# Raw weight blocks of five quads in one ring tile, block by block, with accumulating transfers over two neighbouring quads

## The chip, the cores and the metric

The kernel runs on one core of one Trainium2 chip. The metric is device time in microseconds (us) for one execution; three runs of the kernel before gave 1760.03, 1761.9 and 1763.46, median 1761.9. One more execution was profiled. The five engines of the core are TensorE (PE; its weight loads are PEld), VectorE (DVE), ScalarE (ACT), GpSimd (POOL) and SyncE (SP); each runs its own instructions in order. POOL and SP also issue DMAs.

## The reference, cut to what matters

One decoder layer on x of 256 x 2048 in float32. What matters here are the large products with weights, since nearly all of the time is theirs:

```
x = x + 0.5 * (silu(h @ w_gate) * (h @ w_up)) @ w_down      # first FFN, 2048 -> 5632 -> 2048
q, k, v, ... = rmsnorm(x) @ w_in                            # attention and mLSTM, 256 positions
x = x + concat(y_A, y_B) @ w_out
x = x + 0.5 * (silu(h @ w_gate) * (h @ w_up)) @ w_down      # second FFN, the same shapes
out = rmsnorm(x)
```

## The kernel before, in words

**One product.** Every float32 operand is split into a high and a low part: `wh` is a rounded copy made on ACT (L132), `wl` the rest, made on DVE (L133). A block of weights of 128 x 512 is multiplied as high x high, high x low and low x high: two matmuls with `wh` (L181, L182), one with `wl` (L184). The split parts of 1024 columns are one pair of tiles of the pool `wsp`; four pairs are there, so ACT and DVE can be at most four pairs ahead of PE.

**Quads.** `Paired` computes two neighbouring column chunks, `wa` and `wb` (gate and up, or two chunks of the down projection), over the same activations. For its first `ns` pairs of 128 rows it takes seven products for the eight of a 2 x 2 block of weights, a *quad*, by sums of blocks. A quad holds three raw blocks of 128 x 512: block 0 is the first row block of `wa`, blocks 1 and 2 are the two row blocks of `wb`; the second row block of `wa` comes later, as `late` (L511), for two quads at once. The sums:

- T1 (L479, DVE): block 0 becomes block 0 + block 1, block 1 becomes block 2 + block 1, in one instruction.
- T2 (L495, or L497): block 0 becomes block 0 + block 2.
- T3 (L533): block 0 becomes block 0 + `late`.

T3 is always an accumulating DMA from POOL, 128 rows of 2048 bytes for each quad. T2 is one where `by_dma` holds (the gate and up chunks, and the wide ones in the middle of the layer, which have five quads) and its two quads aren't the last ones; otherwise DVE makes it.

**Order.** Quads are handled by twos (`twos`: 0 and 1, 2 and 3, then 4 alone). `leading` loads, splits and multiplies block 0 as it came (A1), makes T1, and for the two quads before splits block 0 again (S1) and makes T2. `sums` then splits block 0 after T2 (S2), issues T3 behind it, multiplies the bare `late` blocks, and the sums in block 1 (S3). `second` takes blocks 0 and 2 of each quad together, after T3. Units of plain products and the work of the chunk before are woven in between. A scheduler places each instruction on its engine by priority; splits and loads have the same high priority, and the engines keep the order in which it put them.

**Queues.** Raw blocks are loaded by POOL (L446 block 0, L208 through `load_pair` blocks 1 and 2 as rows of 4096 bytes; the first chunks by SP), plain units and `late` by SP. A quad's tile is one of five of the pool `wr`, tag `raw`, 6144 bytes in each partition.

Of the kernel before, what the change touches and what calls it, by code (L numbers as in the profile page):

```python
# [9 lines left out]
F32 = mybir.dt.float32  # L10
# [3 lines left out]
ALU = mybir.AluOpType  # L14
# [3 lines left out]
P = 128  # L18
# [6 lines left out]
CW = 512  # L25
# [7 lines left out]
UK = 2  # L33
# [16 lines left out]
ON_POOL = 3  # L50
FIRST_SUMS = 3
FLUSH = 3

SEEDED = N11, N21 = "n11", "n21"

# [5 lines left out]
def tile_trunk_layer(ctx: ExitStack, tc: tile.TileContext, x, xt, par, bias_if, lamv, fnorm,  # L61
                     wg1, wu1, wd1, wqk0, wqk1, wqk2, win, wout, wg2, wu2, wd2, out):
    nc = tc.nc
# [1 line left out]
    big = ctx.enter_context(tc.tile_pool(name="big", bufs=1))  # L65
    slots = ctx.enter_context(tc.tile_pool(name="slots", bufs=22))
    work = ctx.enter_context(tc.tile_pool(name="work", bufs=8))
    wr = ctx.enter_context(tc.tile_pool(name="wr", bufs=5))
    wrp = ctx.enter_context(tc.tile_pool(name="wrp", bufs=5))
    wsp = ctx.enter_context(tc.tile_pool(name="wsp", bufs=4))  # L70
    small = ctx.enter_context(tc.tile_pool(name="small", bufs=2))
    ps_acc = ctx.enter_context(tc.tile_pool(name="ps_acc", bufs=4, space=PSUM))
    ps_tr = ctx.enter_context(tc.tile_pool(name="ps_tr", bufs=2, space=PSUM))

    wqk = [wqk0, wqk1, wqk2]
    uid = [0]

    def nm(s):
        uid[0] += 1
        return f"{s}_{uid[0]}"  # L80
# [69 lines left out]
    def split_weights(src, hi, lo):  # L150
        made = split(src, hi, lo)
        for late, q, past in zip(made, queued, ahead):
            while q and len(splits) >= q[0][0]:
                past.append(q.pop(0)[1])
            del past[:-3]
            for early in past:
                after(late, early)
        return made


    def pair_tiles(pool, tag, shape):
        return (pool.tile(shape, F32R, tag=tag + "h", name=nm(tag + "h")),
                pool.tile(shape, F32R, tag=tag + "l", name=nm(tag + "l")))
# [36 lines left out]
    def flush(n=None):  # L200

        now = pending[:n]
        del pending[:n]
        for f in now:
            f()

    def load_pair(dst, w, k, queue=nc.sync):
        queue.dma_start(dst, w[k // LK][:, k % LK:k % LK + 2, :])  # L208

    def load_unit(w, k, pieces=(UK,), spare=False):  # L210
        n = w.shape[3]
        if spare:
            raw = wr.tile([P, 3, n], F32, tag="raw", name=nm("raw"))[:, 0:UK, :]
        else:
            raw = wrp.tile([P, UK, n], F32, tag="rawp", name=nm("rawp"))
        with tc.high_priority(offset=AHEAD):
            o = k % LK
            for m in pieces:
                nc.sync.dma_start(raw[:, o - k % LK:o - k % LK + m, :], w[k // LK][:, o:o + m, :])
                o += m  # L220
        return raw
# [3 lines left out]
    def in_turn(load):  # L225
        for early in turns[-1:]:
            after(load, early)
        turns.append(load)

    def tile_by_tile(w, ahead):  # L230
        raw = wr.tile([P, 3, w.shape[3]], F32, tag="raw", name=nm("raw"))
        hi, lo = pair_tiles(wsp, "w", [P, UK, w.shape[3]])
        with tc.high_priority(offset=AHEAD):
            for t in range(UK):
                ahead(0, t)
                in_turn(nc.sync.dma_start(raw[:, t, :], w[0][:, t, :]))
                made = split_weights(raw[:, t, :], hi[:, t, :], lo[:, t, :])
        splits.append(made)
        ahead(1)
        return hi, lo  # L240

    def units(accs, xp, w, nk, last_units=1, ahead=None, w0=0, banks=None):
# [16 lines left out]
        for u in range(nu):  # L259
            if u == FLUSH:  # L260
                flush()
# [123 lines left out]
    def wk(name):  # L385
        return work.tile([P, CW], F32, tag="w", name=nm(name))
# [11 lines left out]
    def soon(extra=40):  # L398
        return tc.high_priority(offset=AHEAD + extra)

    class Early:


        def __init__(self, engine):
            self.engine = engine
# [16 lines left out]
    class Paired:  # L422

        def __init__(self, xp, wa, wb, nk, ns, w0=0, queue=nc.gpsimd, by_dma=True):

            self.queue, self.by_dma = queue, by_dma and ns > 3
            self.xp, self.wa, self.wb, self.k0 = xp, wa, wb, w0 * LK
            self.ns, self.rest = ns, range(2 * ns, nk, UK)
            self.twos = [range(j, min(j + 2, ns)) for j in range(0, ns, 2)]

            self.n = wa.shape[3]
            self.off = self.n - wb.shape[3]
            self.raws = []

        def job(self, acc, j, xi, w, wi, first, last, on=False):
            xh, xl = self.xp[j][2 * (xi // 4):][:2]
# [2 lines left out]

        def load(self, j):  # L440
            n, off = self.n, self.off
            raw = wr.tile([P, 3, n], F32, tag="raw", name=nm("raw"))
            self.raws.append(raw)
            k = self.k0 + 2 * j
            with tc.high_priority(offset=AHEAD):
                self.queue.dma_start(raw[:, 0, :], self.wa[k // LK][:, k % LK, :])  # L446
                load_pair(raw[:, 1:3, off:], self.wb, k, self.queue)
                if off:
                    nc.gpsimd.memset(raw[:, 1:3, 0:off], 0.0)
# [38 lines left out]
        def second_sum(self, js):  # L488

            self.part(js, self.d, S1, 0, True, True)  # L490
            with tc.high_priority(offset=AHEAD):
                for j in js:
                    raw = self.raws[j]
                    if self.by_dma and js != self.twos[-1]:
                        nc.gpsimd.dma_start(raw[:, 0, :], raw[:, 2, :], accum_op=ALU.add)  # L495
                    else:
                        nc.vector.tensor_tensor(out=raw[:, 0, :], in0=raw[:, 0, :], in1=raw[:, 2, :], op=ALU.add)  # L497

        def copied(self, src, t, slack=SLACK - 1):
# [21 lines left out]
        def sums(self, gently):  # L521

            ds = self.copied(self.d, wk("ds"))
            lates = []
            for js in self.twos:
                lates.append((js, self.late(js)))
                self.part(js, self.x, S2, 0)
                if gently or self.rest[0] // UK not in self.xp:
                    with tc.issue_after(newest[0].ins):
                        flush(1)  # L530
                with tc.high_priority(offset=AHEAD):
                    for i, j in enumerate(js):
                        nc.gpsimd.dma_start(self.raws[j][:, 0, :], lates[-1][1][:, i, :], accum_op=ALU.add)  # L533
                if js[-1] == self.ns - 1:
                    us = self.copied(self.x, wk("us"))
                    with soon():
                        ahead_of_splits(1, nc.vector.tensor_tensor(out=self.d, in0=self.d, in1=us, op=ALU.subtract))
                if len(lates) > 1:
                    self.bare(*lates.pop(0))
            for js, raw in lates:  # L540
                self.bare(js, raw)
            for js in self.twos:
                self.part(js, self.x, S3, 1)
            self.n21 = self.copied(self.x, seeded(N21), SLACK - 2)
            with soon():
                ahead_of_splits(1, nc.vector.tensor_tensor(out=self.x, in0=ds, in1=self.x, op=ALU.subtract))
# [492 lines left out]
    for hb in range(NT):  # L1039
        for h in range(NH):  # L1040
            i = hb * NH + h
# [226 lines left out]
```

## Time and profile before

| | |
|---|---|
| median of three runs | 1761.9 us |
| the profiled execution | 1759.56 us |
| its span, first to last instruction | 1757.8 us |
| PE busy | 1744.6 us, 99% |
| DVE busy | 1617.8 us, 92% |
| ACT busy | 1267.4 us, 72% |
| POOL busy | 429.3 us, 24% |
| queue of POOL's DMAs, share of the 16 DMA engines | 45.1% |
| queue of SP's DMAs, share of the 16 DMA engines | 38.0% |

The first rows are from the times, the others from the profile's page. Busy time counts an instruction's own time; matmuls overlap, so a busy PE is not PE at its peak. PE's clock was granted in full (0.999 of it over the run).

### The profile page before, as it was taken

To read this page: it belongs to the slowest core of one execution; us is meant where nothing else is said; L and a number is where in the kernel's file an instruction comes from. 1 tells how busy PE (TensorE), PEld (TensorE's weight loads), DVE (VectorE), ACT (ScalarE), POOL (GpSimd) and SP (SyncE) were. 2 spreads that over 40 slices of the span, in tenths; PEclk is the share of its full clock that TensorE was granted. 3 is DMA by queue.
4 is the path that set the end of the run, shared out by engine and by line. 5 is a ranking of instruction groups with operands and counts; after the bars stand their busy time and mean duration, and the time that the engine had idled before them with its cause. 6 is when DMAs were issued, how large, how long until landed. Compare 5 with 4: busy or idle time off the path is not lost.

```text
span 1757.8 us, 24486 instructions
## 1 busy us (share of the span) xinstructions
PE 1744.6 (99%) x7926; PEld 1437.7 (82%) x7926; DVE 1617.8 (92%) x2189; ACT 1267.4 (72%) x1949; POOL 429.3 (24%) x630
## 2 busy tenths in 40 slices
PE   9999999999999999999999999999999999999998
PEld 7788888888888888987888888888888878888886
DVE  7999999999999999898888999999999999999997
ACT  8666777777677768777687777776777677677765
POOL 0022332322233312012231101122332332233310
PEclk9999999999999999999999999999999999999999
DMA  9787998999799977577886667898998999799973
GB/s 365 251 254 209 259 261 265 253 292 265 218 262 258 263 252 204 185 230 221 236 238 192 209 210 211 260 265 233 258 260 268 241 268 276 232 246 256 283 254 115
DMA packets 155265, 429.72 MB, mean 244 GB/s; under 512 B 17632, under 2 KB 18944, under 8 KB 154880
## 3 DMA queue, kind: packets, MB, share of 16 engines
q0 software_dynamic: 76304, 196.66, 45.1%
q1 hardware_dynamic: 77680, 229.40, 38.0%
q10 hardware_dynamic: 1152, 2.09, 0.3%
q8 instruction: 62, 1.02, 0.2%
q14 instruction: 67, 0.55, 0.1%
HBM read 349.56 MB, written 2.10 MB: 200 GB/s over the span
## 4 chain that ended last, share of the span: by engine, by line
PE 93%; DMA 2%; DVE 2%; issue 1%; ACT 0%; POOL 0%; SPq 0%; POOLq 0%; DVEq 0%; ACTq 0%
PE acc L184 18%; PE acc L181 18%; PE acc L182 18%; PE accn L181 12%; PE accn L182 12%; PE accn L184 12%; DVE wl L133 1%; DMA raw<-in_wg_dram 1%; PE tr L373 1%; DMA raw<-in_wu_dram 1%; PE tr L314 0%; PE sc L1060 0%; DMA rawp<-in_wg_dram 0%; ACT wh L132 0%; PE num L1011 0%
## 5 line engine op out<-in xcount | busy, mean ns | idle before, releaser
L132 ACT CAST wh<-raw 128x512 fp32r<-128x512 f32 (+2 forms) x885 | 601.5, 708 | 214.5 <-PE acc L182 66.3
L133 DVE TENSOR_TENSOR wl<-raw,wh 128x512 fp32r<-128x512 f32 (+2 forms) x885 | 676.1, 793 | 58.4 <-ACT wh L132 54.5
L132 ACT CAST wh<-rawp 128x1024 fp32r<-128x1024 f32 (+3 forms) x308 | 318.2, 1035 | 109.5 <-PE acc L182 55.1
L133 DVE TENSOR_TENSOR wl<-rawp,wh 128x1024 fp32r<-128x1024 f32 (+3 forms) x308 | 367.1, 1197 | 32.0 <-ACT wh L132 29.8
L181 PE MATMUL acc<-wh,xs 128*128 128x512 f32 (+2 forms) x956 | 369.5, 387 | 0.0
L182 PE MATMUL acc<-wh,xs 128*128 128x512 f32 (+2 forms) x956 | 368.9, 386 | 0.0
L184 PE MATMUL acc<-wl,xs 128*128 128x512 f32 (+2 forms) x956 | 317.6, 387 | 0.8 <-DVE wl L133 0.7
L533 POOL DMA_DIRECT2D raw<-late x176 | 152.6, 1053 | 442.7 <-DVE wl L133 422.9
L181 PE MATMUL acc<-wh,xt 128*128 128x512 f32 (+2 forms) x564 | 218.4, 388 | 0.7 <-ACT wh L132 0.7
L182 PE MATMUL acc<-wh,xt 128*128 128x512 f32 (+2 forms) x564 | 217.3, 386 | 0.0
L181 PE MATMUL accn<-wh,xt 128*128 128x512 f32 (+1 forms) x552 | 215.3, 391 | 0.0
L182 PE MATMUL accn<-wh,xt 128*128 128x512 f32 (+1 forms) x552 | 214.7, 390 | 0.0
L479 DVE TENSOR_TENSOR raw<-raw 128x1024 f32<-128x1024 f32 x176 | 211.0, 1217 | 0.8
L184 PEld LDWEIGHTS acc<-wl,xs 128*128 128x128 f32 x956 | 178.3, 188 | 39.2 <-DVE wl L133 3.6
L181 PEld LDWEIGHTS acc<-wh,xs 128*128 128x128 f32 x956 | 179.5, 188 | 36.4 <-ACT wh L132 0.6
L182 PEld LDWEIGHTS acc<-wh,xs 128*128 128x128 f32 x956 | 179.6, 188 | 35.6
L181 PE MATMUL accn<-wh,xs 128*128 128x512 f32 (+1 forms) x408 | 162.6, 400 | 1.9 <-ACT wh L132 1.9
L182 PE MATMUL accn<-wh,xs 128*128 128x512 f32 (+1 forms) x408 | 158.0, 388 | 0.0
L184 PE MATMUL acc<-wl,xt 128*128 128x512 f32 (+2 forms) x564 | 157.6, 386 | 0.0
L495 POOL DMA_DIRECT2D raw<-raw x92 | 78.9, 899 | 322.1 <-DVE wl L133 234.7
L184 PE MATMUL accn<-wl,xt 128*128 128x512 f32 (+1 forms) x552 | 154.7, 388 | 0.0
L184 PE MATMUL accn<-wl,xs 128*128 128x512 f32 (+1 forms) x408 | 140.9, 388 | 0.0
(229 smaller groups left out, 2125.0 us busy)
## 6 DMA issues: line engine op xcount, KB each, us to landing
rawp<-in_wd_dram SPq DMA_DIRECT2D x88, 512.0 KB, 5.6
raw<-late POOLq DMA_DIRECT2D x174, 256.0 KB, 5.3
raw<-in_wu_dram POOLq DMA_DIRECT2D x80, 512.0 KB, 8.4
rawp<-in_wu_dram SPq DMA_DIRECT2D x73, 512.0 KB, 5.1
rawp<-in_wg_dram SPq DMA_DIRECT2D x69, 512.0 KB, 5.2
raw<-raw POOLq DMA_DIRECT2D x92, 256.0 KB, 4.1
raw<-in_wd_dram POOLq DMA_DIRECT2D x44, 512.0 KB, 8.6
late<-in_wg_dram SPq DMA_DIRECT2D x41, 512.0 KB, 9.2
```

Of the source, the lines that this page charges most:

```text
L132: return (nc.scalar.copy(hi, src), nc.vector.tensor_tensor(out=lo, in0=src, in1=hi.bitcast(F32), op=ALU.subtract))
L133: nc.vector.tensor_tensor(out=lo, in0=src, in1=hi.bitcast(F32), op=ALU.subtract))
L181: nc.tensor.matmul(acc, lh, rh, start=first, stop=False, skip_group_check=on)
L182: nc.tensor.matmul(acc, ll, rh, start=False, stop=False, skip_group_check=on)
L184: newest[:] = [nc.tensor.matmul(acc, lh, rl, start=False, stop=last, skip_group_check=on)]
L373: nc.tensor.transpose(tr[:, i, hb * P:(hb + 1) * P], hs[hb][:, k * P:(k + 1) * P], ident)
L479: nc.vector.tensor_tensor(out=raw[:, 0:2, :], in0=raw[:, 0:3:2, :], in1=raw[:, 1:2, :].to_broadcast([P, 2, n]), op=ALU.add)
L495: nc.gpsimd.dma_start(raw[:, 0, :], raw[:, 2, :], accum_op=ALU.add)
L533: nc.gpsimd.dma_start(self.raws[j][:, 0, :], lates[-1][1][:, i, :], accum_op=ALU.add)
```

## The change

The five tiles of `wr` become one tile `ring` of [128, 3, 5, 512]: all five blocks 0 lie behind each other, then the five blocks 1, then the five blocks 2. A counter gives each quad the next of five places. A quad is a strided view of the ring. Two quads in neighbouring places have their blocks 0 in one stretch of 4096 bytes, and so their blocks 2; `late` of two quads is such a stretch already. Where the places of two quads follow each other, T2 and T3 of both are one accumulating DMA; where the first of them has place 4 and the second place 0, they stay two. The load of blocks 1 and 2 still reads 4096 bytes in a row, but writes two rows of 2048 bytes.

```diff
-    wr = ctx.enter_context(tc.tile_pool(name="wr", bufs=5))
+    wr = ctx.enter_context(tc.tile_pool(name="wr", bufs=1))
+    ring = wr.tile([P, 3, RAWS, CW], F32, name="ring")
+    turn = [0]
+    def raw_place():
+        turn[0] += 1
+        return (turn[0] - 1) % RAWS
+    def raw_tile(n):
+        return ring[:, :, raw_place(), 0:n]
...
+        def added(self, js, dst, srcs):
+            p = self.places[js[0]]
+            if len(js) == 2 and self.places[js[1]] == p + 1:
+                nc.gpsimd.dma_start(ring[:, dst, p:p + 2, 0:self.n], srcs, accum_op=ALU.add)
+            else:
+                for i, j in enumerate(js):
+                    nc.gpsimd.dma_start(self.raws[j][:, dst, :], srcs[:, i, :], accum_op=ALU.add)
...
-                    if self.by_dma and js != self.twos[-1]:
-                        nc.gpsimd.dma_start(raw[:, 0, :], raw[:, 2, :], accum_op=ALU.add)
+                if self.by_dma and js != self.twos[-1]:
+                    p, q = (self.places[j] for j in js)
+                    if q == p + 1:
+                        self.added(js, 0, ring[:, 2, p:p + 2, 0:self.n])
...
-                    for i, j in enumerate(js):
-                        nc.gpsimd.dma_start(self.raws[j][:, 0, :], lates[-1][1][:, i, :], accum_op=ALU.add)
+                    self.added(js, 0, lates[-1][1])
```

In the built program 34 of the 46 twos of T2 become one DMA, and 51 twos of T3; 24 DMAs of T2 and 74 of T3 stay as they were. POOL issues 85 DMAs fewer, 514 for 599. The other engines keep their instructions.

On POOL, one gate and up chunk of the first FFN, from the last loads of its quads to its last T3 (the numbers behind raw and late are tiles). Before:

```order
L446 DMA raw_2266<-in_wg_dram 128x512
L208 DMA raw_2266<-in_wu_dram 128x1024
L495 DMA raw_2176<-raw_2176 128x512
L495 DMA raw_2179<-raw_2179 128x512
L495 DMA raw_2214<-raw_2214 128x512
L495 DMA raw_2217<-raw_2217 128x512
L533 DMA raw_2176<-late_2323 128x512
L533 DMA raw_2179<-late_2323 128x512
L533 DMA raw_2214<-late_2339 128x512
L533 DMA raw_2217<-late_2339 128x512
L533 DMA raw_2266<-late_2365 128x512
```

and now:

```order
L470 DMA ring<-in_wg_dram 128x512
L221 DMA ring<-in_wu_dram 128x2x512
L452 DMA ring<-ring 128x1024 x2
L452 DMA ring<-late_2286 128x1024
L452 DMA ring<-late_2301 128x1024
L455 DMA ring<-late_2326 128x512
```

Each two of T2 and of T3 is one instruction, behind the split of its second quad.

On DVE, a chunk of the second FFN, where the low parts for S2 are made (the last `wl` of the four is that of the second two's second quad; xs is a low part of activations, sg a step of the gate). Before:

```order
L133 TENSOR_TENSOR wl_14017<-raw_13867,wh_14016 128x512
L133 TENSOR_TENSOR wl_14017<-raw_13870,wh_14016 128x512
L133 TENSOR_TENSOR wl_14033<-raw_13905,wh_14032 128x512
L133 TENSOR_TENSOR xs_13782<-xsum_13778,xs_13782 128x512
L395 SCALAR_TENSOR_TENSOR sg_13861<-acc_13469,rstd_10608,sg_13861 128x512
L133 TENSOR_TENSOR wl_14033<-raw_13908,wh_14032 128x512
```

and now:

```order
L146 TENSOR_TENSOR wl_13791<-ring,wh_13790 128x512 x2
L146 TENSOR_TENSOR xs_13563<-xsum_13559,xs_13563 128x512
L146 TENSOR_TENSOR wl_13806<-ring,wh_13805 128x512
L408 SCALAR_TENSOR_TENSOR sg_13642<-acc_13259,rstd_10452,sg_13642 128x512
L146 TENSOR_TENSOR wl_13806<-ring,wh_13805 128x512
```

The third `wl` and the step on xs have changed places; this is so in four chunks, and nowhere else has DVE's order changed. PE and ACT keep theirs. On SP two loads of plain units in the second chunk of the program stand behind two loads of raw blocks instead of ahead of them.

## Rows read from the trace of the kernel before

**Rows 1.** Busy time by stretch: length, then PE, PEld, DVE, ACT, POOL; clock, DMA share, GB/s.

```profile
60.00:1700.00 1640.00, 1639.24 (x7472) 1353.99 (x7472) 1523.40 (x2043) 1188.04 (x1820) 419.86 (x608) 1.00 0.85 245
```

**Rows 2.** POOL's timeline, one gate and up chunk: start, us, instruction, idle before and releaser.

```profile
237.17 0.86 POOL L495 DMA_DIRECT2D raw<-raw  x1 [0.86 <-DVE wl L133]
239.50 0.85 POOL L495 DMA_DIRECT2D raw<-raw  x1 [1.48 <-DVE wl L133]
241.24 0.84 POOL L495 DMA_DIRECT2D raw<-raw  x1 [0.89 <-DVE wl L133]
244.56 3.46 POOL L533 DMA_DIRECT2D raw<-late  x4 [2.48 <-DVE wl L133]
```

**Rows 3.** ACT's timeline, the same chunk.

```profile
242.44 1.14 ACT L132 CAST wh<-raw 128x512 fp32r<-128x512 f32 x2
243.79 0.63 ACT L132 CAST wh<-raw 128x512 fp32r<-128x512 f32 x1 [0.21 <-DMA raw<-raw]
244.32 0.58 ACT L503 COPY ds<-acc 128x512 f32<-128x512 f32 x1
244.99 0.62 ACT L132 CAST wh<-raw 128x512 fp32r<-128x512 f32 x1
...
253.62 1.05 ACT L132 CAST wh<-raw 128x1024 fp32r<-128x1024 f32 x1
```

**Rows 4.** DVE's timeline, the same chunk.

```profile
248.71 0.68 DVE L133 TENSOR_TENSOR wl<-raw,wh 128x512 fp32r<-128x512 f32 x1
```

**Rows 5.** PE's timeline, the same chunk.

```profile
250.19 0.39 PE L184 MATMUL acc<-wl,xs 128*128 128x512 f32 x1
```

**Rows 6.** All T2 by DMA (L495): us from issue to landing.

```profile
DMA to landing us min/median/max: 3.3/4.1/8.2
```

**Rows 7.** DMA queues: packets, MB, share of 16 engines.

```profile
q0 software_dynamic: 76304, 196.66, 45.1%
q1 hardware_dynamic: 77680, 229.40, 38.0%
```

**Rows 8.** Loads by L208 on POOL: duration ns min/median/max, first and last start.

```profile
L208 POOL DMA_DIRECT2D raw<-in_wu_dram x80: 530/537/571, 150.2 to 1631.7; - x80
...
L208 POOL DMA_DIRECT2D raw<-in_wqk_dram x2: 714/728/741, 643.3 to 645.6; - x2
```

**Rows 9.** POOL, ACT, DVE and PE timelines, a chunk at 1110 us.

```profile
1111.12 0.86 POOL L495 DMA_DIRECT2D raw<-raw  x1 [0.90 <-DVE wl L133]
...
1116.27 0.62 ACT L132 CAST wh<-raw 128x512 fp32r<-128x512 f32 x1 [0.15 <-DMA raw<-raw]
...
1119.99 0.68 DVE L133 TENSOR_TENSOR wl<-raw,wh 128x512 fp32r<-128x512 f32 x1
...
1120.87 0.39 PE L184 MATMUL acc<-wl,xs 128*128 128x512 f32 x1
```

**Rows 10.** The same four timelines, a chunk at 1420 us.

```profile
1421.38 0.84 POOL L495 DMA_DIRECT2D raw<-raw  x1 [0.89 <-DVE wl L133]
...
1426.26 0.62 ACT L132 CAST wh<-raw 128x512 fp32r<-128x512 f32 x1 [1.20 <-DMA raw<-raw]
...
1429.97 0.68 DVE L133 TENSOR_TENSOR wl<-raw,wh 128x512 fp32r<-128x512 f32 x1
...
1430.71 0.50 PE L184 MATMUL acc<-wl,xs 128*128 128x512 f32 x1
```

**Rows 11.** POOL, DVE and PE timelines, a chunk at 1462 us.

```profile
1462.59 0.85 POOL L495 DMA_DIRECT2D raw<-raw  x1 [0.90 <-DVE xsum L344]
...
1467.50 0.75 DVE L395 SCALAR_TENSOR_TENSOR sg<-acc,rstd,sg 128x512 f32<-128x512 f32 x1
1468.16 0.68 DVE L133 TENSOR_TENSOR wl<-raw,wh 128x512 fp32r<-128x512 f32 x1
...
1469.42 1.22 DVE L133 TENSOR_TENSOR wl<-late,wh 128x1024 fp32r<-128x1024 f32 x1
...
1471.03 0.61 PE L184 MATMUL accn<-wl,xs 128*128 128x512 f32 x2
```

More of the change, by code (lines that the diff above doesn't have):

```diff
@@ L52 @@
 FLUSH = 3
+RAWS = 5
 SEEDED = N11, N21 = "n11", "n21"
@@ L212, in load_unit @@
         if spare:
-            raw = wr.tile([P, 3, n], F32, tag="raw", name=nm("raw"))[:, 0:UK, :]
+            raw = raw_tile(n)[:, 0:UK, :]
         else:
@@ L230, in tile_by_tile @@
     def tile_by_tile(w, ahead):
-        raw = wr.tile([P, 3, w.shape[3]], F32, tag="raw", name=nm("raw"))
+        raw = raw_tile(w.shape[3])
         hi, lo = pair_tiles(wsp, "w", [P, UK, w.shape[3]])
@@ L432, in __init__ @@
             self.off = self.n - wb.shape[3]
-            self.raws = []
+            self.raws, self.places = [], []
+        def added(self, js, dst, srcs):
[5 more added lines that the diff above has]
+                    nc.gpsimd.dma_start(self.raws[j][:, dst, :], srcs[:, i, :], accum_op=ALU.add)
         def job(self, acc, j, xi, w, wi, first, last, on=False):
@@ L441, in load @@
             n, off = self.n, self.off
-            raw = wr.tile([P, 3, n], F32, tag="raw", name=nm("raw"))
+            place = raw_place()
+            raw = ring[:, :, place, 0:n]
             self.raws.append(raw)
+            self.places.append(place)
             k = self.k0 + 2 * j
@@ L491, in second_sum @@
             with tc.high_priority(offset=AHEAD):
-                for j in js:
-                    raw = self.raws[j]
-                    if self.by_dma and js != self.twos[-1]:
-                        nc.gpsimd.dma_start(raw[:, 0, :], raw[:, 2, :], accum_op=ALU.add)
-                    else:
+                if self.by_dma and js != self.twos[-1]:
+                    p, q = (self.places[j] for j in js)
+                    if q == p + 1:
+                        self.added(js, 0, ring[:, 2, p:p + 2, 0:self.n])
+                    else:
+                        for j in js:
+                            nc.gpsimd.dma_start(self.raws[j][:, 0, :], self.raws[j][:, 2, :], accum_op=ALU.add)
+                else:
+                    for j in js:
+                        raw = self.raws[j]
                         nc.vector.tensor_tensor(out=raw[:, 0, :], in0=raw[:, 0, :], in1=raw[:, 2, :], op=ALU.add)
```

## The prediction

> **What bounds the kernel now.** I read the busy times by stretch first, then the timelines of POOL, ACT, DVE and PE around T2. Between 60 and 1700 us PE is busy 1639.24 of 1640 us [rows 1]: less than 0.8 us of the body is PE standing idle by that row, so nothing that speeds up a transfer can gain much there. What can be lost is open: DVE is busy 1523.40 us of the same stretch, 93%, and the DMA engines 85%. The kernel is PE with two feeders that have little in hand. So the question is where the change makes PE's operands later by more than PE's margin at that place. The head up to 60 us and the end from 1700 us hold no T2 by DMA.
>
> Margin here means the time from the end of a split on DVE to the start of the matmul that reads it. In the chunk of [rows 2 to 5] the low part of the fifth quad ends at 248.71 + 0.68 = 249.39 and PE takes it at 250.19: 0.80 us.
>
> **T2, the term that counts.** Before, T2 of the second two is two DMAs: quad 2's goes out at 239.50, quad 3's at 241.24, behind the splits that they wait for [rows 2]. ACT casts quad 2 at 243.79, just after its T2 has landed (ACT had stood 0.21 us for it), copies ds, and casts quad 3 at 244.99, 3.75 us after that quad's issue [rows 3]. Now one DMA goes out where quad 3's went, and both casts wait for all of it. If it lands X after its issue, quad 2's cast starts at 241.24 + X, ds 0.53 behind it, quad 3's cast another 0.58 (ds's own time) later, at 242.35 + X, where it started at 244.99. Everything behind it on ACT and DVE, which work through one queue here, moves by X - 2.64.
>
> This holds as ordering in any case: each 128x512 piece had a landing of its own, and quad 2's cast followed that one [rows 3]. The Trainium skill, page "DMA: Bandwidth & Descriptors", section "Why a DMA increments its semaphore by 16 and not by 1", states that only the full count tells that all data has landed; by that rule a merged transfer hands over neither quad before both are there, and the trace, where each cast follows a landing of its own piece, agrees as far as it goes.
>
> **X is not in the trace.** A lone T2 of 256 KB takes 3.3 us at best [rows 6], 0.85 of it POOL's issue [rows 2]. The second 256 KB adds between nothing, X = 3.3, and its full moving time. That time follows from the queues [rows 7]. SP's queue, plain copies, took 38.0% of 16 engines for 1757.8 us, 10,688 engine-us for 229.40 MB: 46.6 per MB. POOL's took 12,684 for 196.66 MB; its 151 quads of loads, 118.7 MB, at the copies' rate make 5,530, and 7,154 are left for the 76.5 MB of accumulating pieces: 93.5 per MB, twice a copy. 256 KB are then 0.262 x 93.5 / 16 = 1.53 us, and X = 4.8. Longer rows can save only what is fixed for each row, so I stay nearer to the upper end: X = 4.4, an estimate. Below 3.3 is excluded, since more bytes are moved.
>
> With X = 4.4 the splits move by 1.76 us; less the margin of 0.80, PE stalls 0.96, say 0.9. The same chunk of the second FFN (1601 to 1617 us) has the same shape: together **1.8 us**.
>
> In two chunks T2 already runs among other transfers. Quad 3's cast starts 1116.27 - 1111.12 = 5.15 us after the issue in one [rows 9], 4.88 in the other [rows 10]. The bytes are the same, so I leave the landing where it is; but quad 2's cast and ds, 1.11 us, now come behind it. The margins are 1120.87 - 1120.67 = 0.20 and 1430.71 - 1430.65 = 0.06 us: **1.9 us** together.
>
> In two more the scheduler has put the step on xs ahead of quad 2's split on DVE, so that it fills part of the wait. There the transfer lands at 1462.59 + 4.4 = 1466.99, quad 2's split starts 0.66 later (a cast and a little), then the step on the gate, and quad 3's split starts at about 1468.9 where it stood at 1468.16: 0.75 later, against a margin of 1471.03 - 1470.64 = 0.39 [rows 11]. **0.7 us** for both.
>
> Of the 23 chunks with T2 by DMA 19 have their second two merged. The other 13 have margins of a few us or land under contention; I allow **0.5 us** for all of them and for T3. Sum of the losses 4.9 us.
>
> **Edits at nothing.** T2 of the first two goes out at 237.17 and would land at 241.57; its cast starts at 242.44 [rows 2, 3]. If X were 5.3 this cover would be gone, and ACT would wait there too. T3: four issues from 244.56 on [rows 2], the first cast that reads a result at 253.62 [rows 3]; the merged first two would land near 250, so 3 us are to spare. With two quads in a chunk the cover is thinner; that is in the allowance. POOL: the load of blocks 1 and 2 has 256 rows to write, and the nearest row, the load of two rows of 1536 bytes, takes 728 ns for 537 [rows 8]: 151 x 0.19 = 29 us more. The 85 issues less save 85 x 0.85 = 72 us. POOL idles most of the time [rows 1], so neither reaches the end; a load is late by 0.19 us at most. On SP two loads move behind two others in the second chunk, well ahead of their use. Waits for a quad's place stay with the same instructions of DVE, so no load goes out earlier or later because the tile is one.
>
> **What comes back.** 85 merged transfers move 44.6 MB. If longer rows cost as little as copies they save 47 engine-us per MB, 130 us of all 16 engines; at X = 4.4 it is 0.43 us each, 37 us. Loads and `late` then land a little sooner, where PE now idles 0.76 us in the whole body [rows 1]. I give back 0.7 us.
>
> Sum: 4.9 - 0.7 = +4.2 us. The profiled execution, 1759.56 us (1.76 us around the span of 1757.8), would be 1763.8; the median of the runs lies 2.3 us above it, so the forecast is 1766 us.
>
> **Rivals.**
> *The long rows are cheap.* X near 3.3, a whole 512 KB in the time of 256 KB. Then quad 3's cast moves by 0.66 us, within 0.80; the two plain chunks and the two with xs lose nothing, the crowded ones perhaps 0.25 each: +0.5 - 0.7, 1761.7 us, not slower. It decides below X = 3.44, where 2.64 + 0.80 is. For it: an accumulated byte costs twice a copied one [rows 7], so there is something to save. Against: the bytes must still be read, added and written.
> The Trainium skill's fit in the same page, section "Anatomy of one DMA", is about 2.0 us fixed plus bytes at 436 GB/s: 256 KB more would add 0.6 us, and by that the estimate is X = 3.9, +1.2 to +1.5 us in all, about 1763 us; the lone T2's 3.3 us [rows 6] against the fit's 2.6 shows that it is for plain copies.
> *Relief wins.* Fewer engine-us let every load land sooner, and T2's delay vanishes among margins: bounded by PE's idle time and what hides under overlapping matmuls, -1.5 us at most, 1760.4 us. Against: T2 lies in a queue with 0.2 us in hand, loads have several.
> *The change doesn't do what it says.* The descriptors cut accumulated rows back to 2048 bytes: the packets stay, only the joint wait is left. X = 4.8, 0.4 us more in each of six chunks, and no relief: +7.3, 1769 us.
> *The joint transfer lands late.* Everything behind POOL's issue doubles, X = 0.85 + 2 x 2.45 = 5.75: six chunks lose 1.35 us more, and most of the other 13 begin to lose, say 0.3 each: +16, 1778 us.
>
> **How the numbers follow.** Chances: forecast 0.42, long rows cheap 0.25, relief 0.08, rows cut 0.13, landing late 0.12. A measurement tells 0.2%, 3.5 us, from no change. The forecast's own spread (X from 4.1 to 4.7) is 1764 to 1768, across the bound of 1765.4: 0.27 of it beyond, 0.15 within. Slower by over 0.2%: 0.27 + 0.13 + 0.12 = 0.52. Faster: 0.05 of relief and 0.02 of the cheap rows, if PE hides more waiting than I read, 0.07. Within: 0.41. The range reaches from 1760.5, which holds the cheap rows, to 1774, which holds the cut rows and the lower part of the late case.
>
> **What would show it.** In the trace after: T2 of 512 KB with a median near 4.4 us to landing; ACT's idle time before its cast on DMA ring<-ring well over the 0.2 us seen here, up to 2 us a chunk; PE idle time in the body of 4 to 6 us, in those six chunks; the share of POOL's queue down by 1 to 3 points; POOL busy near 390 us. Wrong would be: a landing near 3.5, PE idle unchanged (then the margins hold), or PE losing time at loads instead, which would mean that rows of 2048 bytes on the load's side cost more than nothing.

## The result, and the profile after

The changed kernel takes 1779.87 us (median of four runs, 1778.56 to 1781.45) against 1760.97 us for the kernel before, run beside it: 18.9 us longer, ratio 1.0109, 95% interval 1.0097 to 1.0121. The forecast was 1766 us, range 1760.5 to 1774: the sign was right, the size was not, and the time lies beyond the range. The profiled execution took 1778.56 us, its span is 1776.8 us.

The page and the views of the changed kernel, first the busy times from 60 to 1700 us (columns as in [rows 1]), then the DMA issues of T2 and T3 (count, KB, median us to landing), the two large queues, POOL's issues of the load of blocks 1 and 2 and of the merged T2 (ns min/median/max), and ACT's waits for DMAs that write the ring (us in total, times, longest):

```profile
60.00:1700.00 1640.00, 1631.57 (x7396) 1337.28 (x7395) 1507.14 (x2021) 1170.65 (x1803) 375.22 (x521) 1.00 0.83 243
```

```profile
ring<-late POOLq DMA_DIRECT2D x51, 512.0 KB, 5.0
...
ring<-late POOLq DMA_DIRECT2D x72, 256.0 KB, 5.4
...
ring<-ring POOLq DMA_DIRECT2D x34, 512.0 KB, 5.3
...
ring<-ring POOLq DMA_DIRECT2D x24, 256.0 KB, 4.5
```

```profile
q0 software_dynamic: 64064, 196.66, 43.9%
q1 hardware_dynamic: 81008, 229.40, 37.7%
```

```profile
L221 POOL DMA_DIRECT2D ring<-in_wu_dram x80: 704/714/760, 152.1 to 1650.7; - x80
...
L452 POOL DMA_DIRECT2D ring<-ring x34: 828/848/933, 88.9 to 1665.8; - x34
```

```profile
ACT wh L145 <- DMA ring<-ring: 38.0, 28, 3.0
...
ACT wh L145 <- DMA ring<-late: 6.3, 5, 2.2
```

PE's idle time in the body is 8.4 us where it was 0.76 [rows 1]. A merged T2 lands 5.3 us after its issue, a single one took 4.1 [rows 6]. ACT waits 38.0 us for T2; for the kernel before the same view has 6.6 us in 14 waits, the longest 1.2:

```profile
ACT wh L132 <- DMA raw<-raw: 6.6, 14, 1.2
```

POOL's queue went from 45.1% to 43.9% of 16 engines, and POOL is busy for 386.3 us on the page.

Idle time tells only half of it, since the ends of matmuls are modelled and a short stall reads as a longer matmul (PE's busy time on the page rose by 11.7 us, to 1756.3). PE's matmuls are the same 7926 in the same order in all kernels of this document, so I took the start of the same matmul in two traces and read off where PE falls behind. That gives 19.0 us at the end. The table has that lag by place: ahead of 60 us, and in 28 us from the first T2 of each of the 23 chunks that have T2 by DMA (named by the time of the first T2 in the kernel before; the 1110, 1420 and 1462 of [rows 9 to 11] are those at 1106, 1415 and 1456). The last three columns are kernels of the experiments. Each column is one profiled execution, and such an execution is not the median: that of the layout alone took 1762.42 us, 2.1 under its median, and that with second twos merged 1775.27, 3.2 above. So prices are taken from the medians, and the table tells places.

| place | forecast | the change | layout alone | first twos merged | second twos merged |
|---|---|---|---|---|---|
| head, up to 60 us | 0 | 1.6 | 1.9 | 2.1 | 1.7 |
| 235 and 1601 (plain) | 1.8 | -0.3 | -1.0 | 0.9 | 1.4 |
| 1106 and 1415 (crowded) | 1.9 | 3.3 | 0.1 | 0.2 | 3.8 |
| 1146 and 1456 (with the xs swap) | 0.7 | 3.4 | 0.6 | 0.8 | 1.9 |
| 358, 399 | in the 0.5 | 2.9 | 0.0 | 1.7 | 0.6 |
| 542, 583, 1289, 1375 | in the 0.5 | 3.9 | 0.8 | 2.8 | 3.9 |
| the other 11 chunks | in the 0.5 | 0.3 | 0.0 | 0.1 | 0.9 |
| two-quad chunks, 263 to 313 and 740 to 770 | in the 0.5 | 3.2 | 0.0 | 0.4 | 0.5 |

The worst single place is the chunk at 1415, which the prediction had from [rows 10]. POOL, ACT and PE of the changed kernel there (its clock is some 15 us later by then):

```profile
1432.60 0.93 POOL L452 DMA_DIRECT2D ring<-ring  x1 [10.11 <-DVE wl L146]
1436.68 0.85 POOL L452 DMA_DIRECT2D ring<-ring  x1 [3.15 <-DVE wl L146]
```

```profile
1438.74 1.14 ACT L145 CAST wh<-ring 128x512 fp32r<-128x512 f32 x2 [0.80 <-DMA ring<-ring]
1442.85 0.62 ACT L145 CAST wh<-ring 128x512 fp32r<-128x512 f32 x1 [2.96 <-DMA ring<-ring]
1443.37 0.58 ACT L532 COPY ds<-acc 128x512 f32<-128x512 f32 x1
1443.85 0.62 ACT L145 CAST wh<-ring 128x512 fp32r<-128x512 f32 x1
```

```profile
1443.52 0.50 PE L194 MATMUL acc<-wh,xs 128*128 128x512 f32 x1 [0.89 <-ACT wh L145]
1444.52 0.50 PE L194 MATMUL acc<-wh,xs 128*128 128x512 f32 x1 [0.27 <-ACT wh L145]
1447.04 0.74 PE L197 MATMUL accn<-wl,xs 128*128 128x512 f32 x2 [0.35 <-DVE wl L146]
```

The first two's transfer is issued at 1432.60 and ACT, at 1438.74, still waits 0.80 us for it: the first twos have lost their cover. The second's is issued at 1436.68; the cast of quad 2 starts 6.17 us later, after 2.96 us of idle ACT, and behind it come ds and quad 3's cast. PE waits for each of them in turn: for the cast of quad 2, for that of quad 3, and for the low part of `late` behind them.

Two of the other places. ACT in the head, kernel before and changed kernel:

```profile
29.99 1.91 ACT L744 ACTIVATE junk<-xres 128x2048 bf16<-128x2048 f32 x1
```

```profile
31.79 1.91 ACT L772 ACTIVATE junk<-xres 128x2048 bf16<-128x2048 f32 x1 [1.43 <-DMA xres<-in_x_dram]
```

This is the first square sum of the residual, 1.8 us late, and with it everything that waits for the norm. And ACT and PE behind a merged T3 in a chunk of two quads of the changed kernel:

```profile
288.97 1.05 ACT L145 CAST wh<-ring 128x1024 fp32r<-128x1024 f32 x1 [2.18 <-DMA ring<-late]
```

```profile
290.56 0.50 PE L194 MATMUL accn<-wh,xt 128*128 128x512 f32 x1 [0.64 <-ACT xt L145]
291.93 0.50 PE L195 MATMUL accn<-wh,xt 128*128 128x512 f32 x1 [0.55 <-DVE xt L146]
```

### The profile page after: what moved, and what is told of

Same layout as the page of the kernel before. It is cut to its first block, busy times and chain, and to the rows that moved or that the text cites. A ratio compares the mean times of both kernels' runs of the same rounds, so it can differ in the third digit from the quotient of the medians.

```text
span 1776.8 us, 24185 instructions
## 1 busy us (share of the span) xinstructions
PE 1756.3 (99%) x7926; PEld 1436.8 (81%) x7926; DVE 1617.3 (91%) x2189; ACT 1262.1 (71%) x1949; POOL 386.3 (22%) x545
## 3 DMA queue, kind: packets, MB, share of 16 engines
q0 software_dynamic: 64064, 196.66, 43.9%
## 5 line engine op out<-in xcount | busy, mean ns | idle before, releaser
L145 ACT CAST wh<-ring 128x512 fp32r<-128x512 f32 (+2 forms) x885 | 600.1, 706 | 241.3 <-PE acc L195 65.0
L146 DVE TENSOR_TENSOR wl<-ring,wh 128x512 fp32r<-128x512 f32 (+2 forms) x885 | 676.5, 791 | 80.3 <-ACT wh L145 75.9
L503 DVE TENSOR_TENSOR ring<-ring 128x1024 f32<-128x1024 f32 x176 | 210.9, 1216 | 0.9
L194 PEld LDWEIGHTS accn<-wh,xt 128*128 128x128 f32 x552 | 103.6, 188 | 28.0 <-ACT accn L532 7.3
L194 PEld LDWEIGHTS acc<-wh,xt 128*128 128x128 f32 x564 | 105.9, 188 | 22.3 <-ACT wh L145 1.5
```

The lines of the kernel that those rows point to most:

```text
L145: return (nc.scalar.copy(hi, src), nc.vector.tensor_tensor(out=lo, in0=src, in1=hi.bitcast(F32), op=ALU.subtract))
L146: nc.vector.tensor_tensor(out=lo, in0=src, in1=hi.bitcast(F32), op=ALU.subtract))
L194: nc.tensor.matmul(acc, lh, rh, start=first, stop=False, skip_group_check=on)
L503: nc.vector.tensor_tensor(out=raw[:, 0:2, :], in0=raw[:, 0:3:2, :], in1=raw[:, 1:2, :].to_broadcast([P, 2, n]), op=ALU.add)
```

## The experiments

The times are medians beside the kernel before on the same chip (1760.5 to 1761.1 us there), the ratios with their 95% intervals, about 2 us to either side. All diffs are against the changed kernel unless another is named; PE, ACT and DVE keep the order of the kernel before but for the four xs swaps, which come with a merged T2 in the second two, and one swap of two neighbouring instructions of ACT in the joint issue.

### The layout alone, T3 alone, T2 alone

Edit of the layout alone: neither condition holds, so each T2 and T3 is a DMA of its own.

```diff
-            if len(js) == 2 and self.places[js[1]] == p + 1:
+            if False:
...
-                    if q == p + 1:
+                    if False:
```

> The ring as in the change, but every T2 and T3 is a DMA of its own again (no merged transfer). Theory (the loss of 19 us comes from handing two quads over together): nearly all of it goes away; what stays is the 1.6 us that PE has lost by 47 us of the profiled run of the change, before any merged transfer: 1762 us, at most 1764. Rival A (the layout costs: loads of blocks 1 and 2 write rows of 2048 bytes, POOL takes 714 ns for them where 537 were, all quads share a tile): most of the loss stays, 1770 us or more.

1764.53 us, ratio 1.0020 (1.0011 to 1.0028): 3.5 us are the price of the layout, 15 us that of the merged transfers. The theory holds for the larger part, at the upper end of what it gave the layout.

T3 merged alone:

```diff
-                    if q == p + 1:
+                    if False:
```

> The ring with T3 merged and every T2 a DMA of its own. Theory: in the trace of the change the places where PE falls behind next to a wait on a merged T3 (near 289, 291, 761 and 1354 us) add up to 3.5 us, those next to a merged T2 to some 14: this kernel stands 3 to 5 us above the layout alone, near 1766. Rival B (T3 is as bad as T2, its delays showing up later at T2's places): 8 us or more above the layout alone, 1770 or more. The prediction had T3 at nothing but a share of 0.5 us: within 1 us of the layout alone.

1764.70 us, ratio 1.0026 (1.0017 to 1.0036). The median says nothing above the layout, the ratio 1 us; the prediction's "nothing" is nearer than my theory. Yet its trace loses 2.6 us at the two chunks of two quads, where the layout alone loses 0.0. The two don't contradict each other: the profiled execution, 1767.31 us, is the longest of its ten, 2.6 above the median. Another run below takes it up.

T2 merged alone (T2 as in the change, T3 single; T2's merged DMA no longer goes through `added`, since that is now always single):

```diff
-            if len(js) == 2 and self.places[js[1]] == p + 1:
+            if False:
...
-                        self.added(js, 0, ring[:, 2, p:p + 2, 0:self.n])
+                        nc.gpsimd.dma_start(ring[:, 0, p:p + 2, 0:self.n], ring[:, 2, p:p + 2, 0:self.n], accum_op=ALU.add)
```

> The ring with T2 merged and every T3 a DMA of its own. Theory: some 14 us above the layout alone, near 1776, and with the gain of the T3-only kernel added the two parts make the whole (1780). The prediction, had its sum been right, has about 4 us here (1766). Rival B: T2 and T3 half each, 1771.

1776.60 us, ratio 1.0095 (1.0081 to 1.0109), 12 us above the layout alone. T2 is the bulk.

### First twos, second twos

T2 merged in the first two of a chunk alone, and in the second two alone, each with T3 single (against T2 merged alone):

```diff
-                    if q == p + 1:
+                    if q == p + 1 and js == self.twos[0]:
```

> The ring, T3 single, T2 merged for the first two of a chunk alone (19 to 23 transfers at most; the second twos single). Theory: a merged T2 lands 5.4 us after its issue, which uses up the 0.87 us of cover that a first two has in the plain chunks, so first twos are part of the loss: 4 to 6 us above the layout alone, 1769. The prediction had them at nothing: within 1 us of the layout alone, 1765.

1768.99 us, ratio 1.0043 (1.0031 to 1.0055): 4.5 us above the layout alone. What the prediction had at nothing costs as much as its whole sum.

```diff
-                    if q == p + 1:
+                    if q == p + 1 and js != self.twos[0]:
```

> The ring, T3 single, T2 merged for the second two of a chunk alone (19 transfers). Theory: 7 to 9 us above the layout alone, 1772, and with the first twos it makes the 12 us of all T2. Rival (the prediction's place is right and only its size wrong): all 12 us are here, 1776.

1772.12 us, ratio 1.0066 (1.0054 to 1.0078): 7.6 us above it. The two parts make the 12 us of all T2. The landings differ by place. From the issue list of the kernel with first twos merged (15 transfers) and of that with second twos merged (19):

```profile
ring<-ring POOLq DMA_DIRECT2D x15, 512.0 KB, 5.9
```

```profile
ring<-ring POOLq DMA_DIRECT2D x19, 512.0 KB, 4.7
```

For single transfers of the kernel before, the same grouping of its 92 rows has medians of 3.99 us in first twos and 4.24 in second twos. So a merged transfer adds 1.9 us in the first two and 0.5 in the second. The packets in the two traces tell a part of the reason: from the end of its issue to its landing SP's queue moves 0.45 MB beside a merged transfer of the first two and 0.18 MB beside one of the second (medians); the difference, at the 46.6 engine-us per MB that the prediction worked out for SP's copies, is 0.8 us by estimate, of the 1.2 between 5.9 and 4.7. It isn't all: in the change the same count gives 0.45 and 0.36 MB, for 5.9 and 5.1 us. And merging the first two delays what follows it: with first twos merged the single transfers of the second twos have a median of 5.09 us, so a part of the 4.5 us arises there.

### Joint landing without a longer transfer

The layout alone, with one edge: the cast of the first quad for S2 waits for the second quad's T2 too (`behind(x, y)` makes x wait for y). Against the layout alone:

```diff
-                            nc.gpsimd.dma_start(self.raws[j][:, 0, :], self.raws[j][:, 2, :], accum_op=ALU.add)
+                            self.t2[j] = nc.gpsimd.dma_start(self.raws[j][:, 0, :], self.raws[j][:, 2, :], accum_op=ALU.add)
...
+                        if i < len(waits):
+                            behind(made[0], waits[i])
...
-            t = self.split_two([self.raws[j][:, slot, :] for j in js])
+            waits = ()
+            if xi == S2 and len(js) == 2 and js[1] in self.t2 and self.places[js[1]] == self.places[js[0]] + 1:
+                waits = (self.t2[js[1]],)
+            t = self.split_two([self.raws[j][:, slot, :] for j in js], waits)
```

> The layout alone (all T2 and T3 single, T2 issued quad by quad as before), with one edge more: where the change merges a two's T2, the first quad's cast for S2 also waits for the second quad's T2. That is the joint landing without the later issue and without the longer transfer. Theory (what costs is how late the later quad's sum lands, not that both are handed over together): by the prediction's own formula with the 4.1 us of a lone T2 the later cast moves by 1.5 us, and most margins take that: 2 to 4 us above the layout alone, 1767. Rival (the joint handover itself): most of the 12 us of merged T2, 1774 or more.

1773.17 us, ratio 1.0068 (1.0055 to 1.0080), 8.5 us above the layout alone: nearer to the rival than to the theory. Transfers land as before (4.0 us in the median); only the handover is joint, and two thirds of T2's price are there. Its ACT waits (of an execution of 1768.74 us, the shortest of five):

```profile
ACT wh L145 <- DMA ring<-ring: 20.1, 18, 2.9
```

The same in first twos alone, and in second twos alone (with `!=` for `==`). Against the joint landing in both:

```diff
-            if xi == S2 and len(js) == 2 and js[1] in self.t2 and self.places[js[1]] == self.places[js[0]] + 1:
+            if xi == S2 and len(js) == 2 and js[1] in self.t2 and js == self.twos[0] and self.places[js[1]] == self.places[js[0]] + 1:
```

> As the joint landing without joint issue, but for the first two of a chunk alone. Theory (first twos lose by the length of the merged transfer: a single T2 of the second quad lands 0.9 us ahead of the cast, so waiting for it costs the first quad next to nothing): within 1.5 us of the layout alone, 1765. Rival (the handover of two at once costs there too): 4 us above it, as merged, 1768.5.

1766.75 us, ratio 1.0036 (1.0023 to 1.0050): 2 to 3 us above the layout alone, where merged cost 4.5. It lies between theory and rival and the intervals don't part it from either.

> The same for the second two of a chunk alone. Theory (here the cast of the first quad and the copy of ds, 1.1 us together, fall behind the second quad's landing, in all 19 chunks and not in six): 6 to 8 us above the layout alone, 1771.5, nearly as much as merged. Rival (the prediction's formula with 4.1 us holds, and the earlier 8 us were first twos): 2 to 3 us above it, 1767.

1771.26 us, ratio 1.0054 (1.0040 to 1.0068): 6 to 7 us above it, where merged cost 7.6. The theory holds: in second twos nearly the whole price is the joint handover, at the landing time of a single transfer. DVE's order is that of the kernel before here, so the xs swaps, which come with the merged transfer, are not needed for it. That the longer transfer matters most in first twos is what the medians say (2 to 3 of 4.5 against 6 to 7 of 7.6); the intervals don't show it.

### Joint issue without joint landing

The layout alone, with T2 single, but where the change merges, both DMAs wait for the second quad's split. Against the layout alone:

```diff
-                    if False:
-                        self.added(js, 0, ring[:, 2, p:p + 2, 0:self.n])
+                    if q == p + 1:
+                        for j in js:
+                            made = nc.gpsimd.dma_start(self.raws[j][:, 0, :], self.raws[j][:, 2, :], accum_op=ALU.add)
+                            behind(made, splits[-1][1])
```

> The ring, all T2 and T3 single, but where the change merges a two's T2, both DMAs wait for the split of the second quad and then go out one behind the other: joint issue, landings of their own, rows of 2048 bytes. Theory (the loss comes by the time at which the slower of the two lands after the joint issue, 5.4 us merged; here the first quad's data is there some 4.1 us after it and the second's 5.0): about half of the merged T2's 12 us, 1770. Rival (the joint landing does it all): 1766 at most. Rival (the joint issue does it all): 1776.

1779.22 us, ratio 1.0105 (1.0090 to 1.0120): 14.7 us above the layout alone, no better than merged, and the second rival is right. But the landings are not those of the expectation. In the 34 twos, in the median, the first transfer lands 4.1 us after the joint issue in first twos and 3.8 in second twos, the second one 6.7 and 5.8, where the merged transfer of the change has 5.9 and 5.1 for both quads. POOL's issues and quad 3's cast in the second two of the chunk at 235, the cast 6.4 us after the joint issue where it was 3.75 [rows 2, 3]:

```profile
243.79 1.70 POOL L526 DMA_DIRECT2D ring<-ring  x2 [2.29 <-DVE wl L146]
```

```profile
250.19 0.62 ACT L145 CAST wh<-ring 128x512 fp32r<-128x512 f32 x1 [1.17 <-DMA ring<-ring]
```

Given that both quads have to wait for the second split, one long transfer is no worse than two, and brings the later sum 0.7 to 0.8 us sooner. This run doesn't part the first quad's waiting from the second's later landing; that the waiting is the larger is argued from the joint landing above, where transfers land as before and 8.5 us are lost.

### Rows of 2048 bytes in a merged transfer

The ring lies quad by quad, so that a merged transfer has two rows of 2048 bytes in each partition and a load writes 4096 bytes in a row again:

```diff
-    ring = wr.tile([P, 3, RAWS, CW], F32, name="ring")
+    ring = wr.tile([P, RAWS, 3, CW], F32, name="ring")
...
-        return ring[:, :, raw_place(), 0:n]
+        return ring[:, raw_place(), :, 0:n]
...
-                nc.gpsimd.dma_start(ring[:, dst, p:p + 2, 0:self.n], srcs, accum_op=ALU.add)
+                nc.gpsimd.dma_start(ring[:, p:p + 2, dst, 0:self.n], srcs, accum_op=ALU.add)
...
-                        self.added(js, 0, ring[:, 2, p:p + 2, 0:self.n])
+                        self.added(js, 0, ring[:, p:p + 2, 2, 0:self.n])
```

> All merged as in the change, but the ring lies quad by quad (places outermost, the three blocks of a quad behind each other), so that a merged transfer still is one instruction with one joint landing, in rows of 2048 bytes, and loads write rows of 4096 again. Every engine's order is that of the change. Theory (joint landing, and 512 KB take twice the moving time whatever the rows): 1780, within 3 us of the change, T2 to landing near 5.2 us as there. Rival C (the rows of 4096 bytes do save engine time and hide a part of the loss): 1784 or more, landing 0.4 us or more later. Rival A (rows of 2048 on the load's side cost): 1775 or less.

1795.16 us, ratio 1.0202 (1.0188 to 1.0216): 15 us worse than the change, with the same instructions in the same order. Rival C is right and my theory falls: the long rows are worth 15 us against merging without them; what the change loses, it loses in spite of them. The source view of the merged transfers in this kernel (POOL's issue, ns min/median/max) and its list of issues:

```profile
L452 POOL DMA_DIRECT2D ring<-ring x34: 1167/1190/1230, 88.6 to 1681.7; - x34
```

```profile
ring<-ring POOLq DMA_DIRECT2D x34, 512.0 KB, 6.4
```

The issue takes 0.34 us more than the change's 0.85, and T2 lands 6.4 us after it in place of 5.3 (7.9 for 5.9 in first twos, 5.8 for 5.1 in second ones). If all of the 15 us came by T2's landing, one more us of it would be worth some 14 us here; that is an estimate, since T3's merged transfers have the short rows too, and the loads the long ones.

### What the layout costs

The layout alone with the two loads of xres in their old order:

```diff
-                nc.sync.dma_start(xres[:, hb, :], x[hb * P:(hb + 1) * P, :])
+                halves_x.append(nc.sync.dma_start(xres[:, hb, :], x[hb * P:(hb + 1) * P, :]))
+                if hb:
+                    after(halves_x[1], halves_x[0])
```

> The layout alone with one edge more: the load of the second half of the residual xres stays behind that of the first half on SyncE, as in the kernel before. In the layout alone and in the change the two loads have changed places, ACT's first square sum (of the first half) starts at 32.05 where it started at 29.99, and PE falls behind by 1.9 us at 44 to 47 us. Theory (that swap is the layout's price): 1.5 to 2 us less than the layout alone, 1762.5, within 0.2% of the kernel before, and the first square sum again near 30.0 us. Rival A (rows of 2048 and longer issues on POOL cost 3 us somewhere else): no change, 1764.5.

1763.45 us, ratio 1.0015 (1.0006 to 1.0024). The square sum starts at 30.11 us and PE's lag at 60 us is 0.2 us, as expected; the whole falls by 1.1 us, which alone is too little to be told from nothing. The other way round, the kernel before with the two loads swapped:

```diff
-            hb = u - (KD // UK - NT)
+            hb = KD // UK - 1 - u
```

> The kernel before with one thing changed: the load of the second half of xres is issued ahead of that of the first half, as in the change. Theory (the swap is a price of its own): ACT's first square sum starts near 32.0 instead of 30.0 us, and the whole is 1 to 2 us longer, 1762.5. Rival (margins further on take it up): no change, 1761.

1762.34 us, ratio 1.0013 (1.0004 to 1.0022), lag at 60 us 1.7 us: the swap costs some 2 us by itself, with an interval of 0.7 to 3.9. And the change with the loads in their old order:

> The change with the two loads of xres in the order of before, nothing else. Theory: 1 to 2 us less than the change, 1778.5. Rival (the lag that PE has from the head is slack for the splits further on, and what is not lost there is lost at T2): no change, 1780.

1778.12 us, ratio 1.0103 (1.0089 to 1.0117), 1.75 us under the change. Three pairs of runs agree on 1 to 2 us; the trace has 1.5.

The ring quad by quad with single transfers and the old order of xres, so that all that differs from the kernel before is that the five quads share a tile. Its diff is that of the quad-by-quad ring, both conditions of the layout alone, and the edge on xres:

```diff
+    ring = wr.tile([P, RAWS, 3, CW], F32, name="ring")
...
+            if False:
...
+                    after(halves_x[1], halves_x[0])
```

> One tile, but quad by quad, all T2 and T3 single, and the two loads of xres in the order of the kernel before: rows and durations of all loads are those of before (537 ns on POOL). Theory (what the layout costs beside the swap is the two rows of 2048 bytes of each load): within 1 us of the kernel before, 1761. Rival (one tile for all quads costs by itself, by waits that are not needed): 1763.5, as the block-by-block layout with the same order.

1760.42 us, ratio 0.9998 (0.9989 to 1.0007). One tile costs nothing. Against the block-by-block ring with the same order (1.0015) some 3 us are left for the load's side (its rows of 2048 bytes, or POOL's longer issue for them), an interval that just excludes zero. In the trace of the block-by-block one, PE loses 2.2 and 2.5 us in the chunks at 583 and 1289, 0.6 at 235, and no more elsewhere. Ahead of the first, on POOL and then on ACT, in that kernel:

```profile
577.35 0.71 POOL L221 DMA_DIRECT2D ring<-in_wu_dram  x1 [2.33 <-DMA ring<-in_wu_dram]
```

```profile
578.19 0.62 ACT L145 CAST wh<-ring 128x512 fp32r<-128x512 f32 x1 [2.25 <-DMA ring<-in_wg_dram]
```

A load waits 2.33 us on POOL for the landing of an earlier load, and a cast waits for a load. Waits of loads for loads stand in the kernel before as well (6.7 us in 6, 12.6 in 8 here). But the layout alone, with the same rows, has 5.0 in 6 and loses 0.7 and 0.1 us in those two chunks. So these waits differ by execution, and how the rows cost their 3 us is not shown.

### T3 by size of chunk

T2 merged everywhere, T3 merged in chunks of five quads alone (T2's line as in T2 merged alone):

```diff
-            if len(js) == 2 and self.places[js[1]] == p + 1:
+            if self.ns > 3 and len(js) == 2 and self.places[js[1]] == p + 1:
```

> The change without merged T3 in chunks of two and three quads; in chunks of five T2 and T3 are merged as in the change. Theory (the wait of 2.2 us for a merged T3 near 289 us and its like are in chunks of two quads): 2 to 3 us less than the change, 1777, as with T2 merged alone. Rival (T3 in the chunks of five adds to the merged T2 there): no less than the change, 1780.

1775.96 us, ratio 1.0088 (1.0074 to 1.0102): no more than T2 merged alone, 3.9 us less than the change. Its lag in the two chunks of two quads is 0.5 us, that of the change 3.2. So the last 3 us are T3 in chunks with few quads, beside a merged T2; with T2 single the same T3 showed 0 to 1 us above. T3 in chunks of five costs nothing that these times can show.

## Why the prediction was wrong in size

**The bound.** Right: PE had nothing to gain, relief brought no time. POOL's queue took 1.2 points less (forecast 1 to 3): 204 engine-us by the two pages (0.451 x 1757.8 against 0.439 x 1776.8, times 16), which is 13 us of all 16 engines, a third of the 37 that the prediction worked with. PE did not get it back as time.

**The two plain chunks.** The change seems to lose nothing there (-0.3 us in the table, forecast 1.8), but this is the base. Three kernels on the ring without a merged T2 (the layout alone, T3 alone, the ring quad by quad with single transfers) stand at -1.0 us in these two chunks, a fourth, the layout alone with the old order of xres, at -0.1: the profiled execution of the kernel before lost up to 1.0 us there itself. Against the layout alone the change loses 0.7 us, all at 235. With the old order of xres it loses 1.9 against the layout alone, and 0.9 against the layout in that order. So the working of these two chunks isn't refuted, and what it gives differs by execution. Less waiting for loads is not the reason either. The cast at 235 that waits for a block of wg, in the kernel before, in the change, and in the ring quad by quad with single transfers:

```profile
232.04 0.62 ACT L132 CAST wh<-raw 128x512 fp32r<-128x512 f32 x1 [3.16 <-DMA raw<-in_wg_dram]
```

```profile
231.75 0.62 ACT L145 CAST wh<-ring 128x512 fp32r<-128x512 f32 x1 [1.82 <-DMA ring<-in_wg_dram]
```

```profile
231.56 0.62 ACT L145 CAST wh<-ring 128x512 fp32r<-128x512 f32 x1 [1.61 <-DMA ring<-in_wg_dram]
```

The wait is as short without any merged transfer, and in the layout alone it is 3.17 us, though PE is no later there.

**The mechanism in second twos.** Right: both quads wait for one landing after the second quad's issue, and the cast of quad 2, ds and quad 3's cast come behind it. The joint landing with single transfers shows it at 6 to 7 us without anything else of the change.

**The size of X.** Forecast 4.4; in second twos it is 4.7 when they alone are merged and 5.1 in the change, in first twos 5.9. The step that failed is the base: the 3.3 us at best [rows 6] instead of the median of 4.1 in the same row. What the second 256 KB adds at best is 4.5 - 3.3 = 1.2 us, between the 1.1 that was taken and the 1.53 from the queues; 4.1 + 1.2 is the 5.3 that was measured. By the fit of the Trainium skill, page "DMA: Bandwidth & Descriptors", section "Anatomy of one DMA", the second 256 KB adds 0.6 us, which on the 3.3 of [rows 6] makes an estimate of 3.9 us for the whole; no merged T2 in the trace lands in less than 4.5 us.

**The number of places.** This is the step that cost most. Six chunks were worked out and 0.5 us were allowed "for all of them and for T3". The six lost 6.4 us where the sum had 4.4 ahead of relief; the allowance lost 7.1 us in other chunks and 3.2 at T3. That those had "margins of a few us" was not read row by row: at 358, 399, 542, 583, 1289 and 1375 the change lost 6.8 us. One execution tells little of a single one of them, since kernels without a merged T2 also lose up to 2.5 us at 583 or 1289 in theirs; as a whole it is clear, for T2 merged costs 12 us by the medians where the sum had 4.9.

**First twos at nothing.** Wrong, 4.5 us, spread over the same places as above. The working held one cover, 0.87 us in one plain chunk [rows 3], and said what would end it: X = 5.3. X is 5.9 there.

**T3 at nothing.** Right for chunks of five quads, wrong for those of two: "3 us to spare" was read in a chunk of five, and the thinner cover, named in the same sentence, got no number.

**SyncE's order at nothing.** Wrong, 1 to 2 us. The prediction saw two loads change places in the second chunk. The two loads of xres had changed places too, and since both read `xres<-in_x_dram` no comparison by name shows it. The first square sum needs the half that now comes second, and ACT works in order.

**The loads at nothing.** POOL's load takes 714 ns, near the 728 of [rows 8], and POOL is at 386 us for the 390 forecast. But the layout costs some 1.5 to 3 us beyond the swap, with the reason not settled.

**The rivals.** "The joint transfer lands late" (X = 5.75, 1778 us) came nearest and had 0.12: its X fits first twos. That is luck in part, since its reason, that everything behind the issue doubles (2.45 us more), is not what the landings show (1.2 more at best). "Rows cut to 2048" was priced at X = 4.8 and 1769 us; built as the ring quad by quad, it has 6.4 and 1795. So the value of long rows was underrated too, as was the slope: one us of landing was taken for one us in each of six chunks, and is worth some 14 by the estimate above.

The parts, each above the one ahead of it by the medians: layout 3.5 (the swap 1 to 2 of it), first and second twos 12.1, T3 3.3; together 18.9. Open stay what beside SP's copies makes merged transfers in first twos land 1.9 us later than single ones, how the rest of the layout's price comes about, and the true margins of the chunks in the allowance.

## What to carry to other kernels

Merging transfers of two pieces that become ready one after the other delays the first to the second's readiness. Here the consumer followed closely, and neither 85 issues fewer nor 1.2 points of the queue gave it back; merging what had cover (T3 in the chunks of five) cost nothing that showed. Size such a change by the margin at every place where it happens, by the median landing, and not by the best case of a chunk or two, since where PE is full each place with no margin counts in full. And look at orders down to the addresses: two loads of the same name may have changed places.

## What the runs showed that I had not expected

An accumulating transfer of 512 KB in rows of 4096 bytes is issued in 0.85 us and lands in 4.5 us at best, the same bytes in rows of 2048 in 1.19 and 5.0 us; in the pattern of this kernel the medians are 5.3 and 6.4, and merging in the shorter rows costs 15 us more of the whole. A single transfer of half the bytes, in as many rows, is issued in 0.85 us too. So in these transfers POOL's time for an issue goes by the rows and not by the bytes, as its loads show as well (537 ns for 128 rows to write, 714 for 256, of the same bytes). The DMA engines' time hardly falls with the longer rows: merged in rows of 4096 bytes the queue took 204 engine-us less for 44.6 MB, under 5 per MB of the 93.5 that the prediction worked out.
